# The end of the last plain pair between two block products, a mean one step later, constants and last weights moved

## The chip, the cores and the metric

The kernel runs on one core of a Trainium2 chip. The metric is device time in microseconds (us), the median over runs. TensorE (PE) does the matmuls, VectorE (DVE) and ScalarE (ACT) the element-wise work, GpSimd (POOL) and SyncE (SP) mostly issue transfers; ACT issues some too. Each engine takes its own instructions in a fixed order and waits where one needs the result of another engine.

## What is computed

A decoder trunk of two layers on 512 tokens with 1024 channels, all in float32. Layer 0 has a mixer of causal pooling and a 31-wide convolution with a LayerNorm, layer 1 a latent attention; both are followed by cross-attention into a memory of 256 tokens, and by a gated feed-forward block:

```python
def conv_ffn(h, w_up, conv_w, conv_b, w_down):
    a, g = jnp.split(h @ w_up, 2, axis=-1)          # 1024 -> 2 x 2816
    g = causal_dwconv(g, conv_w) + conv_b            # width 3, over tokens
    return (jax.nn.silu(g) * a) @ w_down             # 2816 -> 1024

def reference(x, mem, ...):
    for l in range(2):
        h = rmsnorm(x, norm_mix_g[l])
        x = x + (pool_conv_mixer(h, ...) if l % 2 == 0 else mla_attention(h, ...))
        x = x + memory_cross_attention(rmsnorm(x, norm_xa_g[l]), rmsnorm(mem, norm_mem_g[l]), ...)
        x = x + conv_ffn(rmsnorm(x, norm_ffn_g[l]), ffn_w_up[l], ffn_conv_w[l], ffn_conv_b[l], ffn_w_down[l])
    return rmsnorm(x, final_norm_g)

def pool_conv_mixer(...):
    ...
    cv = causal_dwconv(gl, dw_w) + dw_b
    yb = jax.nn.silu(layernorm(cv, ln_g, ln_b))      # mean, then variance, over 512 channels
    return jnp.concatenate([ya, yb], axis=-1) @ w_out
```

## The kernel before

Channels lie on the 128 partitions, tokens along the row. The eight tiles x[0] to x[7] of 128 x 512 hold the residual stream. Each float32 matrix product is made of three matmuls (`mm3`, L179 to L181): both operands are split into a high and a low part, and high by high, high by low and low by high are added up in a PSUM bank. ACT makes the high part (names ending in h, such as wh, th, fh, dwh, dh) and VectorE the low part (wl, tl, fl, dwl, dl); so each weight block goes through a transfer, an ACT cast and a VectorE subtraction before TensorE can use it.

**The feed-forward block** (`ffn`) has 22 pairs of column blocks, gate and other. The first five (`PLAIN_PAIRS`) are plain: `run_plain(t)` makes each of their ten tiles from 24 matmuls of 128x512 in a bank "lin". Their right-hand side is the not yet normalised x (hh, hl), and VectorE multiplies the result by the rate rb; then come the convolution (`convolved`: one ACT step L667, two VectorE steps L668 and L669, silu on ACT L670), the product with the other half (L685), and the split into fh and fl.

The other 17 pairs (`paired(i)`) are done by a scheme of seven products of half-size blocks, in the order a11, s1, s2, a12, s3, s4, a22, each of twelve matmuls of 128x256 in three banks "xyz". Between the products ACT and VectorE copy or combine banks (q at L737 and L741, e at L739, g, c). They need normalised operands and their sums and differences (`Operands.fill`): b11 gives bh and bl, the others u, ta, tb and then th and tl. A generator makes these in 32 steps, four (`OPERAND_STEPS`) after each plain tile. `ENTER` and `NEXT` say at which tile or product the weights of a coming pair are loaded, summed (ws) and split.

**The down product** (`down`, called `lower` where it is stepped) adds the finished pairs into x[m]: in groups of four pairs, for each m, four steps k of three 128x512 matmuls in a bank "down". Its weights come as dr and are split into dwh and dwl one tile ahead, at k = 0. One step is taken after every product of the paired pairs. The last group of six pairs is done in halves of 256 tokens by `finale` (banks "fin", weights dh and dl), together with the final norm; in layer 1 its first weights are split when the paired pairs have ended and `lower` still has its last tiles to do.

**The mixer of layer 0** runs as a list of steps among the cross-attention's key and value products. Its LayerNorm (`normalise`) has seven stages: the sum lacc, the mean as a matmul (L962), differences and squares lsq, the rate (st, ssum), its spreading over the partitions, the scaling, the split. `LATE` gives how many steps of the surrounding work lie behind each stage.

**The start** brings x and the first weight blocks; ACT makes hh of each x tile, VectorE hl. The constants con come in two transfers, the second one (225.5 KB) issued by ACT. Four small ACT operations dg (L944) make diagonal matrices of convolution weights. The squares of the natural-order x (nat, L253) give the first rate, which is spread by a matmul rb.

The order on each engine comes from a scheduler that goes by priorities and dependences as it sees them. `tc.keep_in_program_order` pins an instruction behind the one that the code issued before it on the same engine.

Of the kernel before, what the change touches and what calls it, by code (L numbers as in the profile page):

```python
# [58 lines left out]
PACE = (3, 3, 2, 3)  # L59
MEM1_AT = 10  # L60
RB_K = 6
LATE = (1, 4, 1, 3, 1, 4, 1)
FFN_GROUPS = (4, 4, 4, 4, 6)
PLAIN_PAIRS = 5
OPERAND_STEPS = 4
EARLY = 150
HALF = T // 2
KH = KD // 2
# [37 lines left out]
def kernel(ctx: ExitStack, tc: tile.TileContext, a):  # L106
# [16 lines left out]
    def slot(name, dt=F32, shape=(P, T)):  # L123
        return sl.tile(list(shape), dt, tag="s", name=uid(name))
# [7 lines left out]
    def f(t):  # L132
        return t.bitcast(F32)
# [6 lines left out]
    def col(name, i=0, n=1):  # L140
        c = _COLS[name] + i
        return con[:, c:c + n]
# [31 lines left out]
            vec.tensor_tensor(lo[:, :n], raw[:, :n], f(hi[:, :n]), ALU.subtract)  # L174
        return hi, lo

    def mm3(ps, ah, al, bh, bl, first, last, more=False):

        pe.matmul(ps, ah, bh, start=first, stop=False, skip_group_check=more)  # L179
        pe.matmul(ps, ah, bl, start=False, stop=False, skip_group_check=more)  # L180
        pe.matmul(ps, al, bh, start=False, stop=last, skip_group_check=more)  # L181

# [32 lines left out]
    def split_sb(src, name, shape=(P, T)):  # L215
        h = slot(name + "h", F32R, shape)
        l = slot(name + "l", F32R, shape)
        act.copy(h, src)  # L218
        vec.tensor_tensor(l, src, f(h), ALU.subtract)  # L219
        return h, l  # L220
# [389 lines left out]
    def ffn(layer, norm, nxt, extra=None):  # L610
        prod = []
        plain_raw, plain_w = {}, {}
        tiles = 2 * PLAIN_PAIRS

        def weights_of(t):
            return a["ffn_up"][layer, t // 2 + (0 if t % 2 else KF)]

        def load_plain(t):
            if t < tiles:
                plain_raw[t] = load_raw(weights_of(t), D)  # L620

        def split_plain(t):
            if t < tiles:
                raw = plain_raw.pop(t)
                hi, lo = (early_parts if t % 5 < 2 else parts)()
                act.copy(hi, raw)
                low_by_dma(lo, raw, weights_of(t))
                plain_w[t] = hi, lo

        def run_plain(t):  # L630
            load_plain(t + 4)
            split_plain(t + 3)
            for p, what in ENTER.get(t - tiles, ()):
                getattr(pairs[PLAIN_PAIRS + p], what)()
            hi, lo = plain_w.pop(t)
            ps = bank("lin")
            for k in range(KD):
                c = slice(k * P, (k + 1) * P)
                mm3(ps, hi[:, c], lo[:, c], *norm.h[k], k == 0, k == KD - 1)
            return ps  # L640

        pairs = {i: Weights(layer, i) for i in range(PLAIN_PAIRS, KF)}
        with tc.high_priority(offset=EARLY):
            for t in range(2):
                load_plain(t)
                split_plain(t)
        with tc.high_priority(offset=AHEAD):
            load_plain(2)
            split_plain(2)
            load_plain(3)  # L650
        ahead = [run_plain(0)]
        norm.rate()
        ahead.append(run_plain(1))
        rb = norm.wide()
        ops = Operands(norm, rb)
        filling = ops.fill()

        def fill(n):
            for _ in range(n):
                next(filling, None)  # L660

        def w(i, j):
            return col("ffn_conv_w", (layer * 3 + j) * KF + i)

        def convolved(i, g):
            c = slot("c")
            act.activation(c, g, AF.Identity, bias=col("ffn_conv_b", layer * KF + i), scale=w(i, 2))  # L667
            vec.scalar_tensor_tensor(c[:, 1:], g[:, :T - 1], w(i, 1), c[:, 1:], ALU.mult, ALU.add)  # L668
            vec.scalar_tensor_tensor(c[:, 2:], g[:, :T - 2], w(i, 0), c[:, 2:], ALU.mult, ALU.add)  # L669
            act.activation(c, c, AF.Silu)  # L670
            return c

        def plain(i):

            ps = ahead.pop(0) if ahead else run_plain(2 * i)
            if i:
                fill(OPERAND_STEPS)
            g = slot("g")
            vec.tensor_tensor(g, ps, rb, ALU.mult)
            c = convolved(i, g)  # L680
            ps = ahead.pop(0) if ahead else run_plain(2 * i + 1)
            if i:
                fill(OPERAND_STEPS)
            vec.tensor_tensor(g, ps, rb, ALU.mult)
            vec.tensor_tensor(c, c, g, ALU.mult)  # L685
            prod.append(split_sb(c, "f"))

        starts = [sum(FFN_GROUPS[:n]) for n in range(len(FFN_GROUPS) + 1)]

        def down():  # L690

            todo = [(n, m) for n in range(len(FFN_GROUPS) - 1) for m in range(KD)]

            def fetch_w(j):
                if j < len(todo):
                    n, m = todo[j]
                    raw[j] = slot("dr")
                    sp.dma_start(raw[j], a["ffn_down"][layer, m][:, starts[n] * P:starts[n + 1] * P])

            raw = {}  # L700
            fetch_w(0)
            fetch_w(1)
            nextw = split_sb(raw.pop(0), "dw")
            for j, (n, m) in enumerate(todo):
                hi, lo = nextw
                ps = bank("down")
                for k in range(KH):
                    c = slice(k * P, (k + 1) * P)
                    xh, xl = prod[starts[n] + k]
                    mm3(ps, hi[:, c], lo[:, c], xh, xl, k == 0, k == KH - 1)  # L710
                    if k == 0 and j + 1 < len(todo):
                        nextw = split_sb(raw.pop(j + 1), "dw")
                        fetch_w(j + 2)
                    if k == KH - 1:
                        vec.tensor_tensor(x[m], x[m], ps, ALU.add)
                    yield

        lower = down()

        def paired(i):  # L720
            wt = pairs[i]
            ps = [bank("xyz", (P, HALF)) for _ in range(3)]
            seen = set()
            q, e = slot("q"), slot("e")
            g = slot("g")
            c = None
            for name, other, b in SEVEN:
                for p, what in NEXT.get(name, ()):
                    if i + p < KF:
                        getattr(pairs[i + p], what)()  # L730
                hi, lo = wt.v[name]
                for k in range(KH):
                    s = slice(k * P, (k + 1) * P)
                    mm3(ps[b], hi[:, s], lo[:, s], *ops.v[other][k], b not in seen and k == 0, k == KH - 1, b in seen)
                seen.add(b)
                if name == "a11":
                    act.copy(q[:, :HALF], ps[0])  # L737
                elif name == "s1":
                    act.mul(e[:, :HALF], ps[1], -1.0)  # L739
                elif name == "s2":  # L740
                    act.copy(q[:, HALF:], ps[0])  # L741
                elif name == "a12":
                    vec.tensor_tensor(g[:, :HALF], ps[2], q[:, :HALF], ALU.add)
                elif name == "s3":
                    vec.scalar_tensor_tensor(e[:, HALF:], ps[0], -1.0, e[:, :HALF], ALU.mult, ALU.add)
                elif name == "s4":
                    vec.tensor_tensor(g[:, HALF:], ps[1], q[:, HALF:], ALU.add)
                    c = convolved(i, g)
                else:
                    vec.scalar_tensor_tensor(c[:, :HALF], ps[0], -1.0, c[:, :HALF], ALU.mult, ALU.mult)  # L750
                    vec.tensor_tensor(c[:, HALF:], c[:, HALF:], e[:, HALF:], ALU.mult)
                    prod.append(split_sb(c, "f"))
                next(lower, None)

        for i in range(PLAIN_PAIRS):
            plain(i)
        fill(100)
        for i in range(PLAIN_PAIRS, KF):
            paired(i)
        k0 = starts[-2]  # L760
        if nxt is None:
            last = finale(layer, k0, KF - k0)
            next(last)
        for _ in lower:
            pass
        if nxt is None:
            last.send(prod[k0:])
            return
        if extra is not None:
            extra()  # L770
        for m in range(KD):
            residual(linear(a["ffn_down"][layer, m][:, k0 * P:], prod[k0:]), m, nxt)
# [98 lines left out]
    def mixer(norm, nxt):  # L871
# [136 lines left out]
        for n, (kind, i) in enumerate(order):  # L1008
# [4 lines left out]
            else:  # L1013
                wait.append((kind, i, (project if n else opening)(base[kind] + i)))
            if n == 0:
                act.dma_start(con[:, KD:], a["con"][:, KD:])
            if n == 1:
                lin = Linear(a["pc_in"][base[order[2][0]] + order[2][1]], KD)
                lin.load(0)
# [431 lines left out]
```

## Time and profile before

| | us |
|---|---|
| median of 3 runs | 1384.05 |
| lowest and highest run | 1383.0, 1384.88 |
| the profiled execution | 1383.12 |
| its span, first to last instruction | 1381.3 |
| granted TensorE clock, mean over the span | 0.993 |

All starts below are counted from the start of the span. In a row of the timeline stand the start, the duration, the engine, the line, the operation, the tiles out and in, the shape, how many it groups, and in brackets the idle time ahead of it with the instruction that ended it. A duration includes the pipeline of the engine; the throughput of a row of equal instructions is read from the distance between their starts. In a row of waits stand what waited and for whom, with the total, the number of times and the longest.

### The profile page before, as it was taken

To read this page: it belongs to the slowest core of one execution; us is meant where nothing else is said; L and a number is where in the kernel's file an instruction comes from. 1 tells how busy PE (TensorE), PEld (TensorE's weight loads), DVE (VectorE), ACT (ScalarE), POOL (GpSimd) and SP (SyncE) were. 2 spreads that over 40 slices of the span, in tenths; PEclk is the share of its full clock that TensorE was granted. 3 is DMA by queue.
4 is the path that set the end of the run, shared out by engine and by line. 5 is a ranking of instruction groups with operands and counts; after the bars stand their busy time and mean duration, and the time that the engine had idled before them with its cause. 6 is when DMAs were issued, how large, how long until landed. Compare 5 with 4: busy or idle time off the path is not lost.

```text
span 1381.3 us, 20270 instructions
## 1 busy us (share of the span) xinstructions
PE 1352.6 (98%) x7756; PEld 1168.1 (85%) x7756; DVE 1020.0 (74%) x1897; ACT 748.8 (54%) x1264; POOL 52.9 (4%) x71
## 2 busy tenths in 40 slices
PE   8999999999989999999999999999999999999997
PEld 6888978888879999999887776888887899999987
DVE  6999989554787777776869775755549777777765
ACT  6416456445655555554447786644556555555433
POOL 0000000001100000000000000000011000000000
PEclk9999999999999999999999999999999999999999
DMA  9335634118835545553321113321486455555421
GB/s 327 99 104 188 217 104 151 61 38 207 184 91 130 159 124 138 134 137 94 106 81 50 43 47 107 107 77 61 124 188 124 130 132 143 134 136 144 111 73 62
DMA packets 57265, 168.01 MB, mean 122 GB/s; under 512 B 6480, under 2 KB 8144, under 8 KB 57168
## 3 DMA queue, kind: packets, MB, share of 16 engines
q1 hardware_dynamic: 47664, 135.55, 30.6%
q0 software_dynamic: 7776, 28.32, 12.3%
q10 hardware_dynamic: 1728, 2.86, 0.6%
q8 instruction: 60, 0.98, 0.3%
q14 instruction: 37, 0.30, 0.1%
HBM read 162.50 MB, written 4.19 MB: 121 GB/s over the span
## 4 chain that ended last, share of the span: by engine, by line
PE 88%; DVE 8%; ACT 2%; issue 1%; DMA 0%; SPq 0%; DVEq 0%; ACTq 0%
PE lin L179 11%; PE lin L181 11%; PE lin L180 11%; PE xyz L179 8%; PE xyz L180 8%; PE xyz L181 8%; PE down L180 4%; PE down L179 4%; PE down L181 4%; DVE cv L934 3%; PE s L1273 1%; PE mpv L1310 1%; DVE wl L174 1%; PE t L1298 1%; PE vx L180 1%
## 5 line engine op out<-in xcount | busy, mean ns | idle before, releaser
L179 PE MATMUL xyz<-th,wh 128*128 128x256 f32 x816 | 230.8, 284 | 10.6 <-ACT q L737 10.6
L181 PE MATMUL xyz<-th,wl 128*128 128x256 f32 x816 | 231.5, 284 | 0.0
L180 PE MATMUL xyz<-tl,wh 128*128 128x256 f32 x816 | 231.3, 284 | 0.0
L173 ACT CAST wh<-wr 128x1024 fp32r<-128x1024 f32 (+3 forms) x120 | 112.7, 944 | 161.8 <-issue 60.6
L179 PE MATMUL lin<-hh,wh 128*128 128x512 f32 x432 | 171.0, 396 | 5.9 <-ACT hh L286 5.9
L179 PEld LDWEIGHTS xyz<-th,wh 128*128 128x128 f32 x816 | 155.7, 192 | 23.2 <-ACT q L737 14.9
L180 PE MATMUL lin<-hl,wh 128*128 128x512 f32 x432 | 169.7, 393 | 0.0
L181 PE MATMUL lin<-hh,wl 128*128 128x512 f32 x432 | 169.2, 392 | 0.2 <-DVE wl L174 0.2
L180 PEld LDWEIGHTS xyz<-tl,wh 128*128 128x128 f32 x816 | 156.8, 192 | 7.1
L174 DVE TENSOR_TENSOR wl<-wr,wh 128x1024 fp32r<-128x1024 f32 (+3 forms) x120 | 130.1, 1086 | 42.4 <-ACT wh L173 40.9
L181 PEld LDWEIGHTS xyz<-th,wl 128*128 128x128 f32 x816 | 156.7, 192 | 0.0
L565 DVE TENSOR_TENSOR wl<-ws,wh 128x1024 fp32r<-128x1024 f32 x68 | 83.3, 1225 | 61.4 <-ACT wh L564 47.9
L564 ACT CAST wh<-ws 128x1024 fp32r<-128x1024 f32 x68 | 71.3, 1049 | 103.9 <-PE xyz L180 101.3
L179 PE MATMUL down<-fh,dwh 128*128 128x512 f32 x256 | 101.9, 398 | 1.2 <-ACT dwh L218 1.2
L180 PE MATMUL down<-fl,dwh 128*128 128x512 f32 x256 | 102.0, 398 | 0.0
L181 PE MATMUL down<-fh,dwl 128*128 128x512 f32 x256 | 100.5, 393 | 0.5 <-DVE dwl L219 0.5
L179 PEld LDWEIGHTS lin<-hh,wh 128*128 128x128 f32 x432 | 81.6, 189 | 22.3 <-ACT hh L286 6.2
L180 PEld LDWEIGHTS lin<-hl,wh 128*128 128x128 f32 x432 | 81.5, 189 | 18.5 <-DVE hl L287 2.7
L181 PEld LDWEIGHTS lin<-hh,wl 128*128 128x128 f32 x432 | 81.5, 189 | 17.5 <-DVE wl L174 0.6
L167 POOL DMA_DIRECT2D wl<-in_ffn_up x54 | 46.9, 868 | 1058.2 <-ACT wl L166 1058.2
L934 DVE SCALAR_TENSOR_TENSOR cv<-a,con,cv 128x509 f32<-128x509 f32 (+25 forms) x115 | 79.4, 726 | 0.1
L670 ACT ACTIVATE c<-c 128x512 f32<-128x512 f32 x44 | 27.8, 632 | 58.5 <-DVE c L669 58.3
(404 smaller groups left out, 3152.1 us busy)
## 6 DMA issues: line engine op xcount, KB each, us to landing
wr<-in_ffn_up SPq DMA_DIRECT2D x88, 512.0 KB, 4.1
wl<-in_ffn_up POOLq DMA_DIRECT2D x54, 512.0 KB, 5.7
dr<-in_ffn_down SPq DMA_DIRECT2D x64, 256.0 KB, 4.2
wr<-in_xa_wk SPq DMA_DIRECT2D x16, 512.0 KB, 3.5
wr<-in_xa_wv SPq DMA_DIRECT2D x16, 512.0 KB, 4.3
wr<-in_xa_wq SPq DMA_DIRECT2D x16, 512.0 KB, 3.5
wr<-in_xa_wo SPq DMA_DIRECT2D x16, 512.0 KB, 3.5
wr<-in_ffn_down SPq DMA_DIRECT2D x16, 384.0 KB, 3.3
```

The lines of the kernel that those rows point to most:

```text
L167: pool.dma_start(lo, src, accum_op=ALU.add)
L173: act.copy(hi[:, :n], raw[:, :n])
L174: vec.tensor_tensor(lo[:, :n], raw[:, :n], f(hi[:, :n]), ALU.subtract)
L179: pe.matmul(ps, ah, bh, start=first, stop=False, skip_group_check=more)
L180: pe.matmul(ps, ah, bl, start=False, stop=False, skip_group_check=more)
L181: pe.matmul(ps, al, bh, start=False, stop=last, skip_group_check=more)
L564: act.copy(hi[:, :n], raw)
L565: vec.tensor_tensor(lo[:, :n], raw, f(hi[:, :n]), ALU.subtract)
L670: act.activation(c, c, AF.Silu)
L934: vec.scalar_tensor_tensor(cv[i][:, s:], gl[i][:, :T - s], w, cv[i][:, s:], ALU.mult, ALU.add)
L1273: pe.matmul(ps[i], q[:, i * P:(i + 1) * P], k[:, :P * (i + 1)], start=True, stop=True)
L1298: pe.transpose(banks[b][:, c:c + P], prob[n][i][:, j * P:(j + 1) * P], ident)
```

## The change

It has five parts.

1. `plain` makes its operand steps and its ENTER loads in `prepare(t)`, behind the tile's matmuls and evictions, from pair 0 on (before: from pair 1 on, with a rest of steps behind the last pair).
2. The last plain pair, `last_plain(4)`, is cut in three. Its 48 matmuls run where they ran. Its convolution is issued behind the first product (a11) of the first paired pair, pair 5, and its last product and split behind the third (s2). Some of these ACT operations, and the first matmul of each product of pair 5, are pinned.
3. During pair 5 the down product takes 0, 0, 0, 1, 1, 2, 3 steps behind the seven products (`DOWN_STEPS`) instead of one behind each. Its first weights are split behind a11.
4. `finale` loads and splits its first weights only once `lower` is at its last but one tile (j = 30 of 0 to 31), behind the splits of the down tiles' weights.
5. The LayerNorm's mean comes one step later, and one step less lies between the rate and what follows it (`LATE`). The second constants transfer is pinned on ACT to the place where the code issues it.

```diff
-LATE = (1, 4, 1, 3, 1, 4, 1)
+LATE = (2, 4, 1, 3, 1, 3, 1)
+DOWN_STEPS = {"a11": 0, "s1": 0, "s2": 0, "a12": 1, "s3": 1, "s4": 2, "a22": 3}
...
-    def mm3(ps, ah, al, bh, bl, first, last, more=False):
-        pe.matmul(ps, ah, bh, start=first, stop=False, skip_group_check=more)
+    def mm3(ps, ah, al, bh, bl, first, last, more=False, pinned=False):
+        head = pe.matmul(ps, ah, bh, start=first, stop=False, skip_group_check=more)
+        if pinned:
+            tc.keep_in_program_order(head)
...
-            for p, what in ENTER.get(t - tiles, ()):
-                getattr(pairs[PLAIN_PAIRS + p], what)()
...
-        def fill(n):
-            for _ in range(n):
+        def prepare(t):
+            for p, what in ENTER.get(t - tiles, ()):
+                getattr(pairs[PLAIN_PAIRS + p], what)()
+            for _ in range(OPERAND_STEPS):
                 next(filling, None)
...
+        def last_plain(i):
+            a8 = run_plain(2 * i)
+            prepare(2 * i)
+            a9 = run_plain(2 * i + 1)
+            prepare(2 * i + 1)
+            yield
+            g, u = slot("g"), slot("g")
+            vec.tensor_tensor(g, a8, rb, ALU.mult)
+            vec.tensor_tensor(u, a9, rb, ALU.mult)
+            c = convolved(i, g, True)
+            yield
+            vec.tensor_tensor(c, c, u, ALU.mult)
+            h, l = slot("fh", F32R), slot("fl", F32R)
+            tc.keep_in_program_order(act.copy(h, c))
+            vec.tensor_tensor(l, c, f(h), ALU.subtract)
+            prod.append((h, l))
+            yield
...
             nextw = split_sb(raw.pop(0), "dw")
+            yield 0
             for j, (n, m) in enumerate(todo):
...
-                    yield
+                    yield j
...
-                next(lower, None)
+                if i == PLAIN_PAIRS and name in ("a11", "s2"):
+                    if name == "a11":
+                        next(lower)
+                    next(rest)
+                for _ in range(DOWN_STEPS[name] if i == PLAIN_PAIRS else 1):
+                    next(lower, None)
...
-        for i in range(PLAIN_PAIRS):
+        for i in range(PLAIN_PAIRS - 1):
             plain(i)
-        fill(100)
+        rest = last_plain(PLAIN_PAIRS - 1)
+        next(rest)
         for i in range(PLAIN_PAIRS, KF):
             paired(i)
         k0 = starts[-2]
-        if nxt is None:
-            last = finale(layer, k0, KF - k0)
-            next(last)
-        for _ in lower:
-            pass
+        for j in lower:
+            if nxt is None and last is None and j >= (len(FFN_GROUPS) - 1) * KD - 2:
+                last = finale(layer, k0, KF - k0)
+                next(last)
...
             if n == 0:
-                act.dma_start(con[:, KD:], a["con"][:, KD:])
+                tc.keep_in_program_order(act.dma_start(con[:, KD:], a["con"][:, KD:]))
```

Each engine has as many instructions as before; only their order differs. Three places are shown. The first is ACT at the handover from the plain pairs to pair 5 in layer 0. Before (c740 and fh751 belong to the last plain pair; th745 to th749 are the last operands; q756 is pair 5's; dwh764 and dwh767 are weights of the first two down tiles):

```order
L667 ACTIVATE c740_3533<-g739_3531,con_72 128x512
L218 CAST th745_3572<-u736_3523 128x512
L540 ACTIVATE th747_3576<-ta737_3527 128x512
L670 ACTIVATE c740_3533<-c740_3533 128x512
L218 CAST th749_3580<-tb738_3528 128x512
L218 CAST fh751_3586<-c740_3533 128x512
L737 COPY q756_3593<-xyz753_3590 128x256
L218 CAST dwh764_3620<-dr762_3616 128x512
L218 CAST dwh767_3628<-dr763_3618 128x512
L741 COPY q756_3593<-xyz753_3590 128x256
```

Now (th736 to th740 are the last operands, q752 and e753 pair 5's, c764 the last plain pair's; dwh760 the first down tile's; lines have moved by about 30):

```order
L223 CAST th736_3503<-u726_3453 128x512
L545 ACTIVATE th738_3507<-ta727_3457 128x512
L569 CAST wh765_3620<-wr734_3497 128x512
L223 CAST th740_3511<-tb728_3458 128x512
L765 COPY q752_3580<-xyz749_3577 128x256
L223 CAST dwh760_3607<-dr758_3603 128x512
L769 COPY q752_3580<-xyz749_3577 128x256
L569 CAST wh776_3685<-ws775_3682 128x1024
L584 CAST wh1778_3705<-wr767_3624 128x1024
L673 ACTIVATE c764_3615<-g762_3611,con_72 128x512
L767 ACTIVATE e753_3581<-xyz750_3578 128x256
```

The convolution and the split of the last plain pair (c740, fh751 before) stand behind both q copies now, and only one of the two dwh casts is left ahead of them.

The second place is ACT right behind that, up to the end of pair 5. Before (c783 and fh784 are pair 5's result, dwh778 and dwh799 weights of the third and fourth down tile):

```order
L218 CAST dwh778_3715<-dr769_3632 128x512
L166 ACTIVATE wl1782_3722<-wr772_3638 128x1024
L564 CAST wh793_3777<-ws792_3774 128x1024
L667 ACTIVATE c783_3739<-g758_3595,con_72 128x512
L564 CAST wh795_3798<-wr773_3656 128x512
L670 ACTIVATE c783_3739<-c783_3739 128x512
L218 CAST fh784_3761<-c783_3739 128x512
```

Now (c764 and fh769 are the last plain pair's, c780 and fh781 pair 5's; dwh772 and dwh784 are weights of the second and third down tile):

```order
L678 ACTIVATE c764_3615<-c764_3615 128x512
L569 CAST wh794_3778<-ws793_3775 128x1024
L708 CAST fh769_3655<-c764_3615 128x512
L569 CAST wh796_3799<-wr768_3639 128x512
L223 CAST dwh772_3676<-dr759_3605 128x512
L673 ACTIVATE c780_3723<-g754_3582,con_72 128x512
L678 ACTIVATE c780_3723<-c780_3723 128x512
L223 CAST fh781_3749<-c780_3723 128x512
L223 CAST dwh784_3757<-dr774_3680 128x512
```

The second down tile's cast stands behind wh796, a weight of pair 6 now, and the third's behind pair 5's fh781; before, both were ahead of c783.

The third place is ACT where the paired pairs end in layer 1. Before (fh2595 is the last pair's, dwh2608 the last down tile's, dh are the weights of `finale`):

```order
L218 CAST fh2595_13135<-c2594_13113 128x512
L786 CAST dh2598_13144<-wr2597_13142 128x384
L786 CAST dh2599_13145<-wr2597_13142 128x384
L786 CAST dh2603_13154<-wr2602_13152 128x384
L786 CAST dh2604_13155<-wr2602_13152 128x384
L218 CAST dwh2608_13170<-dr2593_13098 128x512
```

Now (fh2597, dwh2600 and dh are the same in their new numbers):

```order
L223 CAST fh2597_13137<-c2596_13115 128x512
L223 CAST dwh2600_13152<-dr2595_13100 128x512
L820 CAST dh2603_13158<-wr2602_13156 128x384
L820 CAST dh2604_13159<-wr2602_13156 128x384
L820 CAST dh2608_13168<-wr2607_13166 128x384
L820 CAST dh2609_13169<-wr2607_13166 128x384
```

The last down tile's cast moved ahead of the four dh casts.

Elsewhere: on ACT the second con transfer stands behind the last hh instead of ahead of the first, and the four dg stand among the squares nat instead of between the hh; on SP the third weight block of the mixer stands behind the eight nat loads; the matmul rb of the first rate stands three matmuls earlier on TensorE, the mean eight matmuls later.

More of the change, by code (lines that the diff above doesn't have):

```diff
@@ L663, in w, with convolved @@
             return col("ffn_conv_w", (layer * 3 + j) * KF + i)
-        def convolved(i, g):
+        def convolved(i, g, pinned=False):
             c = slot("c")
-            act.activation(c, g, AF.Identity, bias=col("ffn_conv_b", layer * KF + i), scale=w(i, 2))
+            ins = act.activation(c, g, AF.Identity, bias=col("ffn_conv_b", layer * KF + i), scale=w(i, 2))
+            if pinned:
+                tc.keep_in_program_order(ins)
             vec.scalar_tensor_tensor(c[:, 1:], g[:, :T - 1], w(i, 1), c[:, 1:], ALU.mult, ALU.add)
@@ L675, in plain @@
             ps = ahead.pop(0) if ahead else run_plain(2 * i)
-            if i:
-                fill(OPERAND_STEPS)
             g = slot("g")
@@ L680, in plain @@
             c = convolved(i, g)
+            prepare(2 * i)
             ps = ahead.pop(0) if ahead else run_plain(2 * i + 1)
-            if i:
-                fill(OPERAND_STEPS)
             vec.tensor_tensor(g, ps, rb, ALU.mult)
@@ L686, in plain @@
             prod.append(split_sb(c, "f"))
+            prepare(2 * i + 1)
+        def last_plain(i):
+            a8 = run_plain(2 * i)
+            prepare(2 * i)
+            a9 = run_plain(2 * i + 1)
+            prepare(2 * i + 1)
+            yield
[10 more added lines that the diff above has]
+            yield
         starts = [sum(FFN_GROUPS[:n]) for n in range(len(FFN_GROUPS) + 1)]
@@ L715, in down @@
                         vec.tensor_tensor(x[m], x[m], ps, ALU.add)
-                    yield
+                    yield j
         lower = down()
+        last = None
         def paired(i):
@@ L733, in paired @@
                     s = slice(k * P, (k + 1) * P)
-                    mm3(ps[b], hi[:, s], lo[:, s], *ops.v[other][k], b not in seen and k == 0, k == KH - 1, b in seen)
+                    mm3(ps[b], hi[:, s], lo[:, s], *ops.v[other][k], b not in seen and k == 0, k == KH - 1, b in seen,
+                        i == PLAIN_PAIRS and k == 0)
                 seen.add(b)
```

## The prediction

> **What bounds the kernel now.** I read the page first, then the waits of TensorE, then the clock by stretches, then the timeline of each place that these named.
>
> ```profile
> PE 1352.6 (98%) x7756; PEld 1168.1 (85%) x7756; DVE 1020.0 (74%) x1897; ACT 748.8 (54%) x1264; POOL 52.9 (4%) x71
> ...
> PE xyz L179 <- ACT q L737: 10.6, 2, 5.4
> ...
> PE mean L962 <- DVE lacc L957: 1.5, 1, 1.5
> PE down L179 <- ACT dwh L218: 1.2, 1, 1.2
> ```
>
> TensorE is busy 98% of the span, and the diff takes no matmul away. So only its idle time, and matmuls that run slowly after idle time, can be won. The rows of waits (total, times, longest) name three places that the change touches. The largest is q at L737, once in each layer.
>
> ```profile
> 395.88 0.28 PE L180 MATMUL xyz<-bl,wh 128*128 128x256 f32 x1
> 396.00 0.28 PE L181 MATMUL xyz<-bh,wl 128*128 128x256 f32 x1
> 401.69 0.58 PE L179 MATMUL xyz<-th,wh 128*128 128x256 f32 x1 [5.42 <-ACT q L737]
> 406.76 0.28 PE L181 MATMUL xyz<-th,wl 128*128 128x256 f32 x1
> ...
> 1330.78 0.39 PE L180 MATMUL down<-fl,dwh 128*128 128x512 f32 x1
> 1331.00 0.39 PE L181 MATMUL down<-fh,dwl 128*128 128x512 f32 x1
> ```
>
> A block matmul (128x256) starts 0.12 us after the one before it, a down matmul (128x512) 0.23. In layer 0, 5.69 us lie between 396.00 and 401.69 where 0.12 would do: 5.57 lost. From 401.69 up to 406.76 start 17 block matmuls and 3 down matmuls, worth 17 x 0.12 + 3 x 0.23 = 2.73 us at the normal spacing; they took 5.07, so 2.34 more. The clock shows why:
>
> ```profile
> 352.00:394.00 42.00, 42.00 (x186) 34.74 (x186) 37.15 (x64) 28.32 (x40) 5.19 (x6) 1.00 0.70 144
> 394.00:407.00 13.00, 7.58 (x39) 6.97 (x38) 10.92 (x21) 5.92 (x11) 0.00 (x0) 0.74 0.40 138
> ...
> 1067.98 0.28 PE L181 MATMUL xyz<-bh,wl 128*128 128x256 f32 x1
> 1073.46 0.58 PE L179 MATMUL xyz<-th,wh 128*128 128x256 f32 x1 [5.20 <-ACT q L737]
> 1079.17 0.28 PE L181 MATMUL xyz<-th,wl 128*128 128x256 f32 x1
> ```
>
> The granted clock (third number from the end) is 1.00 in the plain stretch and 0.74 in the handover. Layer 1 loses 5.48 - 0.12 = 5.36, and then 5.71 - (20 x 0.12 + 3 x 0.23) = 2.62. The handovers cost 7.9 + 8.0 = 15.9 us. After a stop of 5 us the clock stays low for 5 to 6 us more. By the Trainium skill, "TensorE: Matmul & The Clock Gate", section "What's actually happening", the clock falls after an idle window of about 3.4 us; the trace agrees so far, with slow matmuls behind 5.2 and 5.4 us and none behind the 1.5 and 1.2 us waits quoted further down.
>
> ```profile
> 398.68 0.63 ACT L670 ACTIVATE c<-c 128x512 f32<-128x512 f32 x1 [1.11 <-DVE c L669]
> 400.03 0.68 DVE L685 TENSOR_TENSOR c<-c,g 128x512 f32<-128x512 f32 x1
> 400.63 0.68 DVE L219 TENSOR_TENSOR tl<-tb,th 128x512 fp32r<-128x512 f32 x1
> 400.75 0.62 ACT L218 CAST fh<-c 128x512 fp32r<-128x512 f32 x1 [0.93 <-DVE c L685]
> 401.27 0.37 ACT L737 COPY q<-xyz 128x256 f32<-128x256 f32 x1
> 401.54 1.15 ACT L218 CAST dwh<-dr 128x512 fp32r<-128x512 f32 x2
> ```
>
> The q copy is not slow: it stands on ACT behind silu (398.68) and fh (400.75), which wait for VectorE. VectorE works at the end of the last plain pair and at the last operands (tl until 401.31) in turn, 0.60 us from one 128x512 operation to the next.
>
> **The change part by part.**
>
> *Handover.* Six VectorE operations of the last plain pair (two multiplies by rb, two convolution steps, c times u, fl) leave the stretch ahead of the second product: 6 x 0.60 to 0.66, say 3.8 us. The operand steps also begin one pair earlier, into the 42.00 - 37.15 = 4.85 us in which VectorE idles between 352 and 394. The last tl thus ends between 401.31 - 3.8 = 397.5 and 392.7. I laid the rows of after one behind the other with these durations and get 395.8. TensorE needs the last quarter of operands nine block matmuls into the second product, at 396.12 + 1.08 = 397.2. The first q copy then ends near 396.7, needed by the third product at 397.56. Both old waits vanish, and the slow stretch with them. Pins on the first matmul of each product cost nothing, since TensorE has its products in that order now. The down steps are only divided differently (still seven).
>
> The same layout shows two new waits on ACT. First: the weights' cast dwh772 of the second down tile now stands behind wh796, a 128x512 cast into the buffer that the last product a22 reads. If a22 starts at S, its eleventh matmul starts at S + 1.20 and ends 0.28 later, so wh796 starts near S + 1.52. The casts follow each other at about 0.52, as the pair dwh x2 above shows (1.15 for two that last 0.62), so dwh772 runs from S + 2.04 to 2.66 and TensorE goes on at S + 2.70 instead of S + 1.44: 1.26, and 0.11 for the slower first matmul after a stop. Second: dwh784 stands behind fh781, the cast of pair 5's own result. After the last down matmul starts at E, VectorE adds it to x at E + 0.42, then runs the two 128x256 steps on c 0.60 later, 0.33 apart; fh follows 0.51 after the second (1329.20 to 1329.71 in the rows below), so at E + 1.86, and dwh784 ends at E + 3.00. TensorE has twelve block matmuls until E + 0.23 + 1.44 = E + 1.67 and waits until E + 3.04: 1.37, say 1.45 with the first spacing. Together 2.8 per layer; their bounds are 0 (ACT's other work ends sooner than laid out) and 2.8 plus another slow stretch of 2.34 to 2.62. I take 2.8, since every link has a row. Net: 7.9 - 2.8 = 5.1 and 8.0 - 2.8 = 5.2, together **10.3** (bounds 5.3 and 15.9).
>
> The cover that is left is thin in one place: the copy e753, ACT behind the plain pair's convolution, is read near 402.6 where the sixth product needs it at 403.24 by the layout. If it is late, TensorE waits for just that lateness.
>
> *Weights of the end.*
>
> ```profile
> 1329.20 0.41 DVE L751 TENSOR_TENSOR c<-c,e 128x256 f32<-128x256 f32 x1
> 1329.71 0.62 ACT L218 CAST fh<-c 128x512 fp32r<-128x512 f32 x1 [0.88 <-DVE c L751]
> 1330.23 1.75 ACT L786 CAST dh<-wr 128x384 fp32r<-128x384 f32 x4
> 1331.89 0.61 ACT L218 CAST dwh<-dr 128x512 fp32r<-128x512 f32 x1
> 1332.55 0.50 PE L179 MATMUL down<-fh,dwh 128*128 128x512 f32 x1 [1.16 <-ACT dwh L218]
> 1333.44 0.68 DVE L219 TENSOR_TENSOR dwl<-dr,dwh 128x512 fp32r<-128x512 f32 x1
> 1334.18 0.50 PE L181 MATMUL down<-fh,dwl 128*128 128x512 f32 x1 [0.54 <-DVE dwl L219]
> ```
>
> Four dh casts stand ahead of dwh on ACT, and dl ahead of dwl on VectorE. From 1331.00 to 1334.18 start three down and three fin matmuls, worth 3 x 0.23 + 3 x 0.12 = 1.05, in 3.18: 2.13 lost, 2.24 with the slow first spacing behind. In after dwh2600 follows fh directly (1330.23 to 1330.84) and dwl can end by 1331.65, when TensorE needs them at 1331.23 and 1331.69. Gain **2.0** (0.8 to 2.2). The dh casts come 0.6 later; the first fin matmul goes behind the down tile, which covers them.
>
> *The mean one step later.*
>
> ```profile
> 180.20 0.39 PE L181 MATMUL lin<-yah,wl 128*128 128x512 f32 x1
> 181.24 0.68 DVE L957 TENSOR_TENSOR lacc<-lacc,cv 128x512 f32<-128x512 f32 x1
> 182.07 1.10 PE L962 MATMUL mean<-lacc,om 128*128 128x512 f32 x2 [1.47 <-DVE lacc L957]
> 183.23 0.40 PE L180 MATMUL lin<-yal,wh 128*128 128x512 f32 x1
> ...
> 190.49 0.69 DVE L243 TENSOR_REDUCE ssum<-st 128x4 f32<-128x512 f32 x1 [0.41 <-PE st L241]
> ```
>
> From 180.20 to 183.23 are four slots of 0.23 (0.92): 2.11 lost. Eight matmuls (1.8 us) now stand ahead of the mean, so lacc is there at 181.92 before TensorE asks. What is late next is the rest of the LayerNorm chain: it starts about as before, has more x additions in between on VectorE, and one fewer step of four matmuls later on as cover. The row of ssum shows a chain that already answers at once. I subtract 0.9 and take **1.2** (0.2 to 2.1).
>
> *The start.*
>
> ```profile
> 1.19 0.46 ACTq L1016 DMA_DIRECT2D con<-in_con  x1
> 9.95 0.39 ACT L944 ACTIVATE dg<-ident,con 128x128 f32<-128x128 f32 x1
> 10.24 0.71 ACT L286 ACTIVATE hh<-x,con 128x512 fp32r<-128x512 f32 x1
> 13.57 2.93 ACT L173 CAST wh<-wr 128x1024 fp32r<-128x1024 f32 x3
> 15.91 0.50 PE L181 MATMUL lin<-hh,wl 128*128 128x512 f32 x1 [0.21 <-DVE wl L174]
> ...
> wr<-in_ffn_down SPq DMA_DIRECT2D x16, 384.0 KB, 3.3
> ```
>
> Four dg operations leave the gaps between hh, 0.29 each by the step from 9.95 to 10.24: 1.2 us. The issue of con (0.46) now stands ahead of wh instead. So wh, and the wait at 15.91, come 0.74 earlier, more if the x transfers gain from con's absence. Against it: the dg, now among the squares for the first rate, read con. If con needs from 12.8 the 3.3 us of the nearest transfer, it is there at 16.1, and ACT, which wants the first dg near 15.4 (12.83, two of the three casts, and one square), waits 0.7; the first rate is then as late as before while TensorE is earlier, and loses up to 0.4 there. SP issues the third weight behind the natural loads now; it is needed two tiles of 24 matmuls later (48 x 0.23 = 11 us past 15.91), so that costs nothing. I take **0.8** (-0.4 to 1.5).
>
> Sum: 10.3 + 2.0 + 1.2 + 0.8 = 14.3. The profiled execution took 1383.12 (span 1381.3 and 1.8 around it), so 1368.8; the median of the runs, 1384.05, is 0.9 above it: **1369.7**. Best ends: 15.9 + 2.2 + 2.1 + 1.5 = 21.7, so 1362.4. Worst: 5.3 + 0.8 + 0.2 - 0.4 = 5.9, so 1378.2.
>
> **The rivals.**
>
> *No new waits.* ACT reaches dwh772 and dwh784 in time, because a22 starts later or the buffers turn otherwise. Gain 15.9 + 4.0 = 19.9: 1364.2. Against it: wh796 stands ahead of dwh772 in ACT's fixed order and needs a22's eleventh matmul.
>
> *The two short waits drop the clock again.* Two stops of 1.3 us lie within about 5 us. For it: the clock row of 0.74 shows what idle time costs in this stage. Against it: the single stop of 1.47 us is followed by a matmul of 0.40 us (183.23), about as long as an undisturbed one (0.39). Price: 2.34 + 2.62 = 5.0 more: 1374.7. The Trainium skill, "TensorE: Matmul & The Clock Gate", section "A second HAM failure mode: psum-queue depth-cycling", speaks for it: frequent micro-idles between groups of matmuls throttle the clock again. No run here has shown that yet.
>
> *The handover does not move.* VectorE or ACT holds another operand or copy just as long; the stop of about 8 us merely changes its name. Gain 4.0 alone: 1380.0. Against it: 3.8 us of work leave VectorE's path.
>
> *Slower: VectorE is the bound of the stage.* If the operands end no earlier than 401.31, the first stop stays, and the plain pair's end (six operations, 3.8, and ACT's 0.8 and 0.6) comes on top before e753 and the down steps: a second stop of 5.2 and a slow stretch of 2.3 to 2.6, some 7.7 per layer. That is 15.4 - 4.0 = 11.4 more: 1395.5. It turns to a loss once the second stops exceed 2.0 per layer. Against it: 4.85 us of idle time on VectorE ahead.
>
> **How the numbers follow.** Chances: the sum 0.51; no new waits 0.14; the clock 0.21; no move 0.09; slower 0.05. A measurement tells 0.2%, 2.8 us, from no change. The first three are faster (0.86), and of "no move" 0.05 is, with the start and the mean failing in the rest; 0.01 of the last rival falls within 0.2%: faster 0.91, same 0.05, slower 0.04. The range takes in the best end and the clock rival: 1363 to 1376, leaving out 0.14 and little more.
>
> **What would show it.** Right: no wait of xyz for q; a granted clock near 1.00 from the last plain tile to pair 5's end; two waits of 1.2 to 1.4 us of down for dwh in each layer; no wait for mean; no wait for dwh in front of the fin matmuls; the matmul that waited for wl at 15.91 about 0.7 earlier. Wrong: slow matmuls behind the short waits, a wait for e in the sixth product, st or rb of the first layer waiting longer than before.

## The result and the profile after

The changed kernel takes 1372.53 us (median of 4 runs, 1371.83 to 1374.02) against 1384.14 (1383.0 to 1384.88): a ratio of 0.9922, 95% interval 0.9909 to 0.9934, so 11.6 us less. The profiled execution took 1371.83, its span is 1370.1, and its mean granted clock 0.998. The forecast was 1369.7 within 1363 to 1376.

The busy row of the page and the waits of TensorE, after the change (lines have moved: L182, L185 and L186 are the three matmuls of `mm3`):

```profile
PE 1348.3 (98%) x7756; PEld 1163.9 (85%) x7756; DVE 1017.8 (74%) x1897; ACT 748.6 (55%) x1264; POOL 52.8 (4%) x71
...
PE lin L182 <- ACT hh L291: 5.5, 1, 5.5
PE down L182 <- ACT dwh L223: 4.7, 4, 1.2
PE rb L273 <- DVE rxy L239: 1.4, 1, 1.4
PE lin L185 <- DVE hl L292: 0.5, 2, 0.3
PE st L246 <- DVE lsq L1004: 0.5, 1, 0.5
```

The 10.6 us for q are gone, and so are the waits for mean and the ones in front of the fin matmuls. In their place stand four waits of down for dwh, and waits for rb, hl and st in layer 0. The first row is the wait for the first x at the start, as before.

The stretches of the handover in layer 0 (busy time of the engines, then the granted clock):

```profile
394.00:407.00 13.00, 13.00 (x93) 12.21 (x92) 11.85 (x20) 8.08 (x13) 0.86 (x1) 1.00 0.47 136
407.00:420.00 13.00, 10.64 (x70) 9.45 (x69) 9.27 (x16) 5.63 (x10) 0.00 (x0) 1.00 0.61 176
```

TensorE is busy for all 13.00 us where it was for 7.58, at a clock of 1.00 instead of 0.74. The 2.4 us that it lacks in the second stretch are the two new waits. TensorE's rows that show them, in layer 0 and in layer 1, and ACT's rows ahead of them:

```profile
409.68 0.50 PE L182 MATMUL down<-fh,dwh 128*128 128x512 f32 x1 [1.11 <-ACT dwh L223]
416.81 0.50 PE L182 MATMUL down<-fh,dwh 128*128 128x512 f32 x1 [1.24 <-ACT dwh L223]
...
1076.71 0.50 PE L182 MATMUL down<-fh,dwh 128*128 128x512 f32 x1 [1.11 <-ACT dwh L223]
1083.84 0.50 PE L182 MATMUL down<-fh,dwh 128*128 128x512 f32 x1 [1.25 <-ACT dwh L223]
...
408.49 0.62 ACT L569 CAST wh<-wr 128x512 fp32r<-128x512 f32 x1 [0.94 <-PE xyz L185]
409.02 0.61 ACT L223 CAST dwh<-dr 128x512 fp32r<-128x512 f32 x1
...
415.62 0.62 ACT L223 CAST fh<-c 128x512 fp32r<-128x512 f32 x1 [1.87 <-DVE c L779]
416.14 0.61 ACT L223 CAST dwh<-dr 128x512 fp32r<-128x512 f32 x1
```

These are the two links that the prediction laid out: dwh behind a weight cast that waits for a22's eleventh matmul, and dwh behind pair 5's fh. Counted against the normal spacing, as before, they cost 1.38 and 1.51 us in each layer. No slow stretch follows either of them.

The end of the paired pairs in layer 1 (ACT, then TensorE's last down tile):

```profile
1320.61 0.62 ACT L223 CAST fh<-c 128x512 fp32r<-128x512 f32 x1 [0.88 <-DVE c L779]
1321.13 0.62 ACT L223 CAST dwh<-dr 128x512 fp32r<-128x512 f32 x1
1321.65 2.58 ACT L820 CAST dh<-wr 128x384 fp32r<-128x384 f32 x6
...
1322.36 0.39 PE L185 MATMUL down<-fl,dwh 128*128 128x512 f32 x1
1322.61 0.50 PE L186 MATMUL down<-fh,dwl 128*128 128x512 f32 x1
```

dwh follows fh directly, and only 0.02 us and a slower first spacing of 0.1 are left of the 2.24.

The LayerNorm's matmuls, and the one that waits for hl further on:

```profile
182.97 1.02 PE L996 MATMUL mean<-lacc,om 128*128 128x512 f32 x2
190.85 0.66 PE L246 MATMUL st<-ident,lsq 128*128 128x128 f32 x4 [0.47 <-DVE lsq L1004]
...
202.87 1.02 PE L182 MATMUL lin<-ybh,wh 128*128 128x512 f32 x2
...
230.46 0.50 PE L185 MATMUL lin<-hl,wh 128*128 128x512 f32 x1 [0.17 <-DVE hl L292]
```

mean waits for nothing. But st does now, the normalised channels ybh come late (0.40 lost around 202.87), and around 230.46 another 0.74 is lost, where hl of the next norm and a weight come late.

The start (ACT, then TensorE):

```profile
11.53 0.36 ACTq L1050 DMA_DIRECT2D con<-in_con  x1
17.27 0.40 ACT L978 ACTIVATE dg<-ident,con 128x128 f32<-128x128 f32 x1 [1.42 <-DMA con<-in_con]
...
26.62 0.62 PE L273 MATMUL rb<-ident,rxy 128*128 128x128 f32 x4 [1.36 <-DVE rxy L239]
```

The constants land 5.7 us after their issue, ACT stands still for 1.42 us with the squares of the first rate behind it, and rb then waits 1.36 us.

### The profile page after: what moved, and what is told of

Same layout as the page of the kernel before. It is cut to its first block, busy times and chain, and to the rows that moved or that the text cites. A ratio compares the mean times of both kernels' runs of the same rounds, so it can differ in the third digit from the quotient of the medians.

```text
span 1370.1 us, 20267 instructions
## 1 busy us (share of the span) xinstructions
PE 1348.3 (98%) x7756; PEld 1163.9 (85%) x7756; DVE 1017.8 (74%) x1897; ACT 748.6 (55%) x1264; POOL 52.8 (4%) x71
## 4 chain that ended last, share of the span: by engine, by line
PE 87%; DVE 8%; ACT 2%; issue 1%; DMA 1%; SPq 0%; DVEq 0%; ACTq 0%
PE lin L182 11%; PE lin L185 11%; PE lin L186 11%; PE xyz L185 8%; PE xyz L182 8%; PE xyz L186 8%; PE down L182 4%; PE down L185 4%; PE down L186 4%; DVE cv L968 3%; PE s L1307 1%; DVE wl L176 1%; PE mpv L1344 1%; PE t L1332 1%; PE fin L185 1%
## 5 line engine op out<-in xcount | busy, mean ns | idle before, releaser
L186 PE MATMUL xyz<-th,wl 128*128 128x256 f32 x816 | 230.1, 282 | 0.0
L185 PE MATMUL xyz<-tl,wh 128*128 128x256 f32 x816 | 229.7, 282 | 0.0
L182 PE MATMUL xyz<-th,wh 128*128 128x256 f32 x816 | 228.7, 282 | 0.0
L182 PE MATMUL lin<-hh,wh 128*128 128x512 f32 x432 | 170.9, 396 | 5.6 <-ACT hh L291 5.5
L185 PE MATMUL lin<-hl,wh 128*128 128x512 f32 x432 | 169.4, 392 | 0.5 <-DVE hl L292 0.5
L186 PE MATMUL lin<-hh,wl 128*128 128x512 f32 x432 | 169.3, 392 | 0.3 <-DVE wl L176 0.3
L182 PEld LDWEIGHTS xyz<-th,wh 128*128 128x128 f32 x816 | 154.1, 190 | 11.6 <-ACT q L765 3.4
L185 PEld LDWEIGHTS xyz<-tl,wh 128*128 128x128 f32 x816 | 155.1, 190 | 7.0
L186 PEld LDWEIGHTS xyz<-th,wl 128*128 128x128 f32 x816 | 155.1, 190 | 0.0
L182 PE MATMUL down<-fh,dwh 128*128 128x512 f32 x256 | 101.8, 398 | 4.7 <-ACT dwh L223 4.7
L185 PE MATMUL down<-fl,dwh 128*128 128x512 f32 x256 | 101.5, 396 | 0.0
L182 PEld LDWEIGHTS lin<-hh,wh 128*128 128x128 f32 x432 | 81.5, 189 | 22.2 <-ACT hh L291 6.2
L186 PE MATMUL down<-fh,dwl 128*128 128x512 f32 x256 | 100.1, 391 | 0.0
L185 PEld LDWEIGHTS lin<-hl,wh 128*128 128x128 f32 x432 | 81.6, 189 | 18.5 <-DVE hl L292 2.2
L186 PEld LDWEIGHTS lin<-hh,wl 128*128 128x128 f32 x432 | 81.5, 189 | 17.9 <-DVE wl L176 1.2
```

The source lines that it names most:

```text
L182: head = pe.matmul(ps, ah, bh, start=first, stop=False, skip_group_check=more)
```

## The experiments

All are versions of the changed kernel. Two theories are tried on the handover: A, that the plain pair's own end held the q copy back; B, that the late operands did. The medians are told against the kernel before in the same session (1383.21 for the first four, 1383.02 for the next four, 1383.77 for the last three). The interval of each ratio reaches 1.3 to 2.3 us to either side, so smaller differences between two versions are read from their waits and spacing, not from their times.

**The pair whole again.**

```diff
-        rest = last_plain(PLAIN_PAIRS - 1)
-        next(rest)
+        plain(PLAIN_PAIRS - 1)
...
-                    next(rest)
```

> The changed kernel with the last plain pair done whole ahead of pair 5 again; the operand steps still begin at pair 0. Theory A (the pair's own end, ahead of the q copy on ACT, is what held the handover): a stop of about 4 us for q comes back in each layer (q near 402.5 where 398.5 would do), followed by slow matmuls for some 2.4 us if 4 us are enough for the clock; the 1.1 us wait for dwh behind the last product goes, since that cast stands ahead of the weight cast again; the wait behind pair 5's fh stays. About 10 us slower than the changed kernel, near 1382. Theory B (the late operands held it): no stop, within 2 us of the changed kernel's 1372.5.

1381.11 us, ratio 0.9986 (0.9976 to 0.9995): only 2.1 below the kernel before. TensorE and ACT in layer 0, and the clock of that stretch:

```profile
395.72 0.28 PE L182 MATMUL xyz<-bh,wh 128*128 128x256 f32 x1
398.47 0.28 PE L186 MATMUL xyz<-th,wl 128*128 128x256 f32 x1
403.75 0.58 PE L182 MATMUL xyz<-th,wh 128*128 128x256 f32 x1 [5.00 <-ACT q L765]
...
402.81 0.62 ACT L223 CAST fh<-c 128x512 fp32r<-128x512 f32 x1 [0.83 <-DVE c L690]
403.33 0.36 ACT L765 COPY q<-xyz 128x256 f32<-128x256 f32 x1
...
397.32 0.68 DVE L224 TENSOR_TENSOR tl<-tb,th 128x512 fp32r<-128x512 f32 x1
...
394.00:407.00 13.00, 8.00 (x48) 7.49 (x47) 9.98 (x16) 4.62 (x9) 0.00 (x0) 0.78 0.41 142
```

The stop for q is back, one product later than before, 1 us longer than expected, and with the low clock. The operands are early here, though: the last tl ends at 398.00, 2.28 us behind the first matmul of pair 5 (395.72), and still q (403.33) stands behind fh (402.81) on ACT. So early operands alone do not free the handover. The stop and its slow stretch cost 7.2 and 7.7 us by the spacing, against 7.9 and 8.0 in the kernel before.

**The operands late again.**

```diff
-            for _ in range(OPERAND_STEPS):
+            for _ in range(OPERAND_STEPS if t > 1 else 0):
                 next(filling, None)
...
         next(rest)
+        for _ in filling:
+            pass
```

> The changed kernel with the operand steps beginning at pair 1 again and a rest of steps at the end; the last plain pair stays cut. Theory A: the last operands end 1 to 1.5 us late, so a wait of about that length for tl in the second product of each layer, no slow clock: near 1375. Theory B: the stop of 5 us and the slow stretch stay in each layer: near 1387.

1377.92 us, ratio 0.9964 (0.9951 to 0.9977): 5.3 below the kernel before, and 2.9 above what A forecast. TensorE's waits in layer 0 behind the first matmul of pair 5, and VectorE's last operand:

```profile
396.34 0.28 PE L182 MATMUL xyz<-bh,wh 128*128 128x256 f32 x1
398.08 0.39 PE L185 MATMUL xyz<-bl,wh 128*128 128x256 f32 x1 [0.18 <-DVE bl L530]
400.69 0.38 PE L182 MATMUL xyz<-th,wh 128*128 128x256 f32 x1 [1.04 <-ACT th L545]
401.42 0.39 PE L185 MATMUL xyz<-tl,wh 128*128 128x256 f32 x1 [0.34 <-DVE tl L546]
...
406.23 0.50 PE L186 MATMUL down<-fh,dwl 128*128 128x512 f32 x1 [0.51 <-DVE dwl L224]
...
401.88 0.68 DVE L224 TENSOR_TENSOR tl<-tb,th 128x512 fp32r<-128x512 f32 x1
```

There is no stop of 5 us, and the granted clock from 394 to 407 is 1.00, so the cut alone ends the stop and the slow stretch. But the operands end at 402.56, 6.22 us behind pair 5's first matmul, where before the change they ended 6.63 behind it (401.31 and 394.68). They and what VectorE does behind them cost several short waits: 5.9 us lost in layer 0 and 5.8 in layer 1 (in layer 0 2.56 up to the second product, 1.26, 1.38 and 0.72 at the down tiles), against 2.9 in the changed kernel. So both halves are needed: alone they win 0.5 and 2.1 us per layer, together 5.1. What the one frees, the other still blocks.

**The constants early again.**

```diff
-                tc.keep_in_program_order(act.dma_start(con[:, KD:], a["con"][:, KD:]))
+                act.dma_start(con[:, KD:], a["con"][:, KD:])
```

> The changed kernel without the pin on the second constants transfer: it is issued at 1.2 us again, and the four dg stand between the hh. Theory: the 1.4 us wait of rb comes from ACT waiting 1.42 us for the constants ahead of the first dg; without it that wait is gone, and the start is as in the kernel before (hh 0.9 apart, first matmul 0.3 later, the wait for wl at 15.9): net 0.8 faster, near 1371.7. Rival: rb is late because four dg and the third weight's cast changed places with the squares; then a wait of about 1 us stays and the kernel is 0.3 to 0.8 slower than the changed one.

1370.53 us, ratio 0.9909 (0.9894 to 0.9923): 12.7 below the kernel before, where the changed kernel is 11.6 below; 1.1 us is less than the intervals can tell. The wait shows it: rb, here three matmuls later in the order again, waits for nothing:

```profile
25.74 0.60 PE L273 MATMUL rb<-ident,rxy 128*128 128x128 f32 x4
```

**The old LATE table.**

```diff
-LATE = (2, 4, 1, 3, 1, 3, 1)
+LATE = (1, 4, 1, 3, 1, 4, 1)
```

> The changed kernel with the old LATE table. Theory: the mean's 1.5 us wait (2.1 us with the spacing) comes back, and with it go the waits for st (0.6), for the normalised channels (0.4), and for hl near 230 (0.75): within 0.5 us of the changed kernel, 1372.5. Rival: the waits for st and hl have another cause (the shifted start); they stay and the kernel is 1.3 to 2 us slower, near 1374.

1372.11 us, ratio 0.9920 (0.9904 to 0.9937): no difference that can be measured. The mean's wait is back as it was:

```profile
183.68 0.67 PE L996 MATMUL mean<-lacc,om 128*128 128x512 f32 x1 [1.47 <-DVE lacc L991]
```

and st, ybh and hl no longer wait. By the spacing 2.12 us are lost at the mean, where the changed kernel loses 0.41 there, 0.63 at st, 0.40 at ybh and 0.74 at hl: 2.18. The wait was passed on, not removed.

**The down product begun ahead of pair 5.**

```diff
+        next(lower)
         for i in range(PLAIN_PAIRS, KF):
             paired(i)
...
-                    if name == "a11":
-                        next(lower)
```

> The changed kernel with the down product begun (its transfers and first split issued) ahead of pair 5 instead of behind its first product; on ACT the second down tile's cast dwh then stands ahead of the 128x512 weight cast that waits for the last product. Theory: the first new wait (1.38 us of lost slots behind a22 in each layer) is made by that place in ACT's order alone; it goes, the second (1.51) stays: 2.8 us faster than the changed kernel, near 1369.7. Rival: the cast is late anyway (transfer, VectorE's dwl), so the wait only changes its name: within 1 us of 1372.5.

1368.26 us, ratio 0.9893 (0.9878 to 0.9908). The waits of the down tiles are now

```profile
PE down L186 <- DVE dwl L224: 0.6, 1, 0.6
...
PE down L182 <- ACT dwh L223: 0.4, 2, 0.2
...
413.07 0.41 DVE L778 SCALAR_TENSOR_TENSOR c<-xyz,c 128x256 f32<-128x256 f32 x1
413.74 0.68 DVE L741 TENSOR_TENSOR x<-x,down 128x512 f32<-128x512 f32 x1
```

The first wait for dwh is gone, a shorter one for dwl (0.4 and 0.9 us lost) is left, and the second fell from 1.51 to 0.45 as well: VectorE makes pair 5's last two steps on c (413.07) ahead of the addition to x (413.74) here, and behind it in the changed kernel, so fh and the dwh behind it come earlier. By the spacing some 3.6 us of waits are gone where 2.8 were forecast; by the medians, each against its kernel before, the gain over the changed kernel is 3.2 (14.8 and 11.6).

**The down steps ahead of pair 5's end.**

```diff
+                if name == "a22" and i == PLAIN_PAIRS:
+                    for _ in range(DOWN_STEPS[name]):
+                        next(lower, None)
                 if name == "a11":
                     act.copy(q[:, :HALF], ps[0])
...
-                for _ in range(DOWN_STEPS[name] if i == PLAIN_PAIRS else 1):
+                for _ in range((0 if name == "a22" else DOWN_STEPS[name]) if i == PLAIN_PAIRS else 1):
```

> The changed kernel with the three down steps behind a22 issued ahead of pair 5's own end, so that the third down tile's cast stands ahead of silu and fh on ACT. Theory: the second new wait (1.51 us in each layer) is made by that place alone; it goes, the first (1.38) stays: 3.0 us faster than the changed kernel, near 1369.5. Rival: the end of pair 5 comes later in exchange, and a later step (x, q of pair 6) waits: within 1 us of 1372.5.

1369.53 us, ratio 0.9899 (0.9882 to 0.9916). Only the first wait of each layer is left:

```profile
PE down L182 <- ACT dwh L223: 2.2, 2, 1.1
```

So 3.0 us of waits are gone, as forecast; by the medians the gain over the changed kernel is 1.9 (13.5 and 11.6).

**The four dg late.**

```diff
-                act.activation(dg, ident, AF.Identity, scale=...)
+                tc.keep_in_program_order(act.activation(dg, ident, AF.Identity, scale=...))
```

> The changed kernel with the four dg pinned to where the code issues them, far behind the first rate; the second constants transfer stays where the change put it. Theory: rb waited because ACT stood still for the constants ahead of the first dg; the wait of 1.4 us (1.5 with the spacing) goes: near 1371.0, and about level with the kernel that issues the constants early. Rival: the wait comes from the third weight's cast and subtraction having moved behind the squares; it stays, near 1372.5.

1370.79 us, ratio 0.9910 (0.9895 to 0.9924). With the constants where the change put them, rb no longer waits, and the taps wait 0.33 us for a dg:

```profile
25.53 0.62 PE L273 MATMUL rb<-ident,rxy 128*128 128x128 f32 x4
...
96.11 1.07 PE L980 MATMUL tap<-a,dg 128*128 128x482 f32 x2 [0.33 <-ACT dg L979]
```

So rb waited because ACT stood still in front of the dg; the third weight behind the squares was not the cause.

**The last weights ahead of the down tiles again.**

```diff
-        for j in lower:
-            if nxt is None and last is None and j >= (len(FFN_GROUPS) - 1) * KD - 2:
-                last = finale(layer, k0, KF - k0)
-                next(last)
+        if nxt is None:
+            last = finale(layer, k0, KF - k0)
+            next(last)
+        for j in lower:
+            pass
```

> The changed kernel with the weights of the end split ahead of the last down tiles again. Theory: the waits for dwh and dwl (2.24 us of lost slots) come back and nothing else moves: near 1374.8. Rival: without them another wait stood in their place (the first fin matmuls), so less than 1 us comes back.

1374.09 us, ratio 0.9937 (0.9923 to 0.9952). Both waits are back, 2.23 us by the spacing:

```profile
1323.67 0.50 PE L182 MATMUL down<-fh,dwh 128*128 128x512 f32 x1 [1.17 <-ACT dwh L223]
1325.29 0.50 PE L186 MATMUL down<-fh,dwl 128*128 128x512 f32 x1 [0.53 <-DVE dwl L224]
```

**The mends together.** The edits of the early constants, the early down product and the early down steps in one kernel:

> The changed kernel with three things together: the down product begun ahead of pair 5, its three steps behind a22 issued ahead of pair 5's end, and the constants issued early as before the change. Theory: the three losses have separate causes, so the gains add up: 4.3 (measured alone), 3.0 at most 0.9 of which the first has already taken, so 2.0 to 3.0, and 2.0: 8.3 to 9.3 below 1372.5, near 1364. Rival: the gains share a cover (VectorE is busy in the handover), and one of the down casts is late again: 1366 to 1368.

1366.04 us, ratio 0.9874 (0.9859 to 0.9889): 17.7 below the kernel before. Of the down tiles' waits only this is left:

```profile
PE down L186 <- DVE dwl L224: 0.8, 2, 0.4
...
406.28 0.62 ACT L223 CAST dwh<-dr 128x512 fp32r<-128x512 f32 x1
...
408.02 0.68 DVE L224 TENSOR_TENSOR dwl<-dr,dwh 128x512 fp32r<-128x512 f32 x1
```

That is 0.7 us lost per layer by the spacing. dwh is there at 406.90, but VectorE, busy without a pause from 403.47 on, comes to dwl at 408.02 only; so a busy VectorE holds it, as the rival said, though what is late is a subtraction and not a cast. The time lies in the rival's range and 2 us above the 1364 of the theory. Most of that is in how 1364 was reckoned: it set medians of other sessions against 1372.5 (gains of 4.3, 3.0 and 2.0). Each against the kernel before in its own session, the three gain 3.2, 1.9 and 1.1 over the changed kernel, 6.1 together, and the three in one kernel gain 6.1 (17.7 and 11.6). The match is closer than the intervals warrant, the more as the first mend takes a part of the second's wait. In the profiled execution the start lost as much as in the kernel before (10.0 us up to 16 us, its first matmul at 5.95 included), 0.6 more than in the run with the early constants alone.

The same with the dg late instead of the constants early:

> The same with the constants left where the change put them and the four dg pinned late instead. Theory: level with the version that issues the constants early, within 0.7 us, since each takes the wait for rb away and each has a small cost of its own (hh further apart there, a wait of the taps for dg here). Rival: the start's transfers decide, and the early constants cost 0.7 us of x: this one is faster by that.

1366.31 us, ratio 0.9875 (0.9860 to 0.9890), level with the one above.

The changed kernel beside them:

> The changed kernel itself beside the others on the same chip: 1372 to 1373, the two waits of 1.38 and 1.51 in each layer and the wait for rb of 1.3 to 2.0 again, whatever the start of its transfers.

1372.01 us, ratio 0.9919 (0.9903 to 0.9936). The waits for dwh are the same to the hundredth (1.38 and 1.51 by the spacing); rb waits 1.8 instead of 1.4, so the first 30 us vary by some tenths between executions of one kernel. Both mended kernels are 6 us faster than this one.

## Why the prediction came out as it did

The time lay in the range and 2.8 us above the forecast. Term by term, in time lost against the normal spacing:

| term | forecast gain | measured gain | from |
|---|---|---|---|
| handover, two layers | 10.3 | 10.1 | 7.92 + 7.99 - 2 x 2.89 |
| weights of the end | 2.0 | 2.1 | 2.24 - 0.12 |
| the mean | 1.2 | -0.1 | 2.12 - 2.18 |
| the start | 0.8 | -0.8 | 0.74 won up to the matmul of 15.91, 1.52 lost at rb |
| sum | 14.3 | 11.3 | 1383.12 - 1371.83 = 11.3 |

*Handover: the gain right, one link of it not.* The old stop and the slow stretch vanished, and the two new waits came where the layout had put them, at 1.38 and 1.51 for 1.37 and 1.45. The thin cover that the prediction named held: the copy e753 ended at 403.46, and the sixth product began at 404.16. The rival "no new waits" failed on ACT's order, as the two mends showed, which move the down steps and with them the casts. "The handover does not move" and "slower" failed because the operands were early enough:

```profile
395.59 0.28 PE L182 MATMUL xyz<-bh,wh 128*128 128x256 f32 x1
...
397.18 0.68 DVE L224 TENSOR_TENSOR tl<-tb,th 128x512 fp32r<-128x512 f32 x1
```

But they were so by little. The last tl ended at 397.86, and TensorE took it up at 398.10: a cover of 0.2 us, where the layout had 1.4 (395.8 against 397.2). That this link cost nothing is in part luck. The step of it that failed is the 3.8 us of VectorE work that the cut was to take out of the operands' way. Counted from pair 5's first matmul, the last tl ended 6.63 us behind it before the change, 6.22 with the cut alone, and 2.28 both with the early operand steps alone and with both. So the early steps bring the operands forward, and the cut frees the q copy on ACT. By the prediction's 397.5 against 397.2 the cut alone would have left a wait of some 0.3 us; the version with the cut alone lost 2.56 up to the second product, and 5.9 in all.

*The clock: right.* Two waits of 1.1 to 1.25 us within 7.1 us left the clock at 1.00, and so did the row of short waits in the version with late operands (1.00 as well), while the stop of 5.0 us in the version with the whole pair brought it down to 0.78 in its stretch. So the rule of the Trainium skill on micro-idles ("TensorE: Matmul & The Clock Gate", section "A second HAM failure mode: psum-queue depth-cycling") did not bear on this case. Its rule of an idle window of about 3.4 us (the Trainium skill, "TensorE: Matmul & The Clock Gate", section "What's actually happening") agrees with every stop seen here: those of up to 2.0 us left the clock alone and those of 5.0 us and more did not, and no run had one between.

*The end: right.* Its two waits went and nothing came in their place; the version with the old order brought 2.23 us of them back.

*The mean: mis-sized.* The step that failed is "I subtract 0.9". The prediction expected the rest of the LayerNorm chain to come late, and its sign of being wrong showed at st: 0.63 was lost there, 0.40 at ybh, and 0.41 at the mean itself by its own two slow slots. It left out what the shifted LayerNorm pushes back behind itself on VectorE and ACT: the next norm's hl, 0.74. So 2.18 went against the 0.9. With the old table all three go, and the mean's 2.12 come back, so the table is shown to be their cause; which of the moved rows makes hl late was not tried.

*The start: wrong sign.* The step that failed is the landing of con, taken as 3.3 us from the nearest transfer. It took 5.7, so ACT stood for 1.42 us instead of 0.7, although con was issued at 11.53 and not at 12.8, and rb lost 1.52 instead of 0.4. A nearer row stood beside the one that the prediction took, among the transfers of the kernel before: con itself, at its old place among the first loads.

```profile
con<-in_con ACTq DMA_DIRECT2D x1, 225.5 KB, 4.0
```

The forecast bound of -0.4 was too near. The 0.74 us that the matmul of 15.91 was to win did come (it began at 15.17, with as many matmuls ahead of it). The versions with con early and with the dg late show the cause by taking the wait for rb away, each in its own way.

## What to carry to other kernels

Before costing a move, write each engine's new order down and follow the first instruction that waits: here it named the two new waits to a tenth, and the same order showed how to mend them, by issuing the waiting cast one step earlier. Work that is taken off an engine need not bring what stands behind it forward by its length: here 3.8 us less on VectorE brought the operands 0.4 nearer. A wait at a chain's head that is taken away by delaying its consumer can come back further along the same chain, as all of it did here, so count every later stage that loses cover, not only the next. A transfer that moves to a later place must be costed with its landing in that place's load, and whatever stands behind its first reader on that engine.

## What was not expected of the hardware

A transfer of 225.5 KB took 5.7 us from its issue at 11.5 us to the first instruction that could read it, while larger ones of 384 KB take a median of 3.3 us elsewhere. The 256 KB transfers of x and nat in the same stretch took as long (medians of 5.7 and 5.9 us), and the transfer engines are 87% busy in the first 16 us after the change; that this load is the reason was not tried. The slow stretch behind a stop, too, is about as long as the stop here: after stops of 5.0 to 5.4 us the matmuls ran slowly for 4.2 to 5.7 us. The stops of these runs are all of one size, so whether its length follows that of the stop is not shown.
